# The head of a two-layer trunk: its first two output pairs run tile by tile together, and the dt chain moves up behind the sums of squares

## The chip, the cores and the metric

One NeuronCore of a Trainium2 chip runs the whole program. The metric is the device time of one execution in microseconds; the kernel before and the changed one compute the same numbers. Engines go by these names: TensorE (PE in the rows; PEld its weight loads), VectorE (DVE), ScalarE (ACT), GpSimd (POOL) and SyncE (SP, whose queue issues most transfers).

## The reference, cut to what matters

Two residual layers over x, 512 positions by 1024 channels. Layer 0 mixes tokens with a Mamba-2 state-space block, layer 1 with a convolution module; each is followed by a gated MLP. Only the start of layer 0 matters here:

```python
u = rms_norm(h, norm_mix[0])                 # h = x
zxbcdt = u @ in_proj                         # 1024 -> 2048 (z) + 4096 (x, B, C) + 32 (dt)
z, xbc, dt = split(zxbcdt)
xbc = silu(causal_dwconv(xbc, conv_w, conv_b))          # width 4
dt = softplus(dt + dt_bias)
acs = cumsum(dtc * a, axis=1)                # within chunks of 128 positions, a = -exp(a_log)
scores = cb[..., None] * exp(seg) * dtc      # seg: differences of acs, causal
y_diag = einsum(scores, xc); y_off = einsum(cc, state) * exp(acs)
```

The norm's factor rstd is one number for each position, so it can be applied after the product with `in_proj`.

## The kernel before

Channels lie on the 128 partitions and the 512 positions in the free dimension: x is eight tiles of 128x512 (`xin[0..7]`, 256 KB each). Each float32 operand of a large product is split into a rounded half and a remainder, and three matmuls (`L308` to `L310`) stand for one product. x is split by `split_x` (ScalarE makes the high half at L242, VectorE the low half at L243), weights by `Weights._make` (GpSimd the high half at L125, VectorE the low half at L127).

**Units and pairs.** An output pair is two tiles of 128 output channels, each summed in one PSUM bank; the pool of these banks, `mm`, has four. `in_proj` has 24 pairs. A unit `(kind, pair, k)` is the part of a pair that x tiles k and k+1 give: 2 tiles by 2 outputs by 3 matmuls, twelve. Pair `in` 0 has units (0,0), (0,2), (0,4), (0,6), and so on. `weight_units` lists all units in the order of use; `Weights.get` hands them out in that order and makes units up to four ahead. A unit's weights are 256 KB. Two successive units of one pair come in one load of 512 KB, except that the first two units of all are loaded alone. The loads land in `wraw` (three buffers), the split halves lie in `whi` and `wlo` (five buffers each).

**The head.** SP issues, in this order: tile 0, unit 0's weights, tile 1, unit 1's weights, tiles 2 and 3, the weights up to unit 3, tiles 4 to 7, the weights up to unit 5, then five constants (`dtw`, `parc`, `con`, `dtp`, `par`). All x tiles are split and squared (`SqSum.add`, the sum on VectorE at L285). Then the loop over eight head groups g starts. In group 0 it runs pair 0 (B and C of the group), pair 1 (the group's x) and pair 2 (its z), one after the other.

**The sums and rstd.** `start_rstd` (called in the hook behind pair 0's fourth unit) issues the dt products (sixteen records, eight tiles) into the bank `dps` (L357), then `SqSum.rstd`: the sum of squares is split in two (L239, L240), two products with ones add it over the channels (L294, L295), a root (L297) and a reciprocal on VectorE (L298) give `rstd`.

**Freeing a bank.** `scaled` multiplies a bank by rstd into a `u` tile (L337; six `u` tiles in all), which frees the bank. `conv4` then makes the convolution from `u` into `cv` tiles (L429, L433, L439; eight `cv` tiles, which also hold x at the start).

**The dt chain.** `dt_chain` (called behind pair 1's convolution) multiplies `dps` by rstd (L371, into a `u` tile), folds its four partial sums with a product on TensorE (L373), and then goes back and forth between VectorE and ScalarE on 32 partitions: v (L378), absolute value, exponential, o (L383), logarithm (L385), L386, L387, dt (L389), the scan to `acs` (L395), `nac`, and the decay weights (L407 to L409). Six of its results are `u` tiles: dv, v, e, o, dt and nac. On SP it issues the writes of `acs`, `nac` and `dec` to DRAM and the read back of `dec`. `dt_transposes` and the first `load_acs` (both in group 1's first hook) use what it leaves; `core` of group 0 has four stages, of which `stage_a` needs the loaded `ab` and makes exponentials from it, `stage_b` multiplies with them on TensorE (L509), and `stage_c` multiplies with the states (L532).

**What sets the order.** The program's order gives each instruction its rank; a planner lays out the order on each engine from it, and takes a later instruction first where by its own times an earlier one is not ready. The order on an engine is then fixed, and semaphores make each instruction wait for its operands. A tile's buffer is given out by the same planner.

Of the kernel before, what the change touches and what calls it, by code (L numbers as in the profile page):

```python
# [20 lines left out]
KD = D // P  # L21
NG = 8
# [20 lines left out]
    _n += _w  # L43
NCOL = _n

KINDS = {"in": KD, "out": DI // P, "up0": KD, "dn0": NF, "pw1": KD, "pw2": KD, "up1": KD, "dn1": NF}


def weight_units():
    seq = []  # L50

    def pair(kind, p, k0=0, k1=None):
        k1 = KINDS[kind] if k1 is None else k1
        seq.extend((kind, p, k) for k in range(k0, k1, 2))

    def two(kind, p, k0, k1):
        for k in range(k0, k1, 4):
            for q in (p, p + 1):
                seq.extend((kind, q, kk) for kk in range(k, min(k + 4, k1), 2))

    for g in range(NG):
        pair("in", 3 * g)
        if g == 5:
            for p in range(4):
                pair("out", p, 0, 8)
        pair("in", 3 * g + 1)
        if g != 1:
            pair("in", 3 * max(g - 1, 0) + 2)
    pair("in", 3 * 7 + 2)
    two("out", 0, 8, 16)  # L70
    pair("out", 2, 8, 16)
    pair("out", 3, 8, 16)

    def ffn(i):
        for a, b in FPARTS:
            for p in range(a, b):
                pair(f"up{i}", p)
            for p in range(4):
                pair(f"dn{i}", p, a, b)

    ffn(0)
    for p in range(8):
        pair("pw1", p)
    two("pw2", 0, 0, 8)
    pair("pw2", 2)
    pair("pw2", 3)
    ffn(1)
    return seq
# [54 lines left out]
def trunk(ctx, tc, a, out):  # L143
    nc = tc.nc
# [13 lines left out]
    W = Weights(tc, nc, a, wr, ws, 4)  # L158
# [10 lines left out]
    def mm_tile():  # L169
        return pm.tile([P, T], F32, name="mm", tag="mm")  # L170
# [25 lines left out]
    xin = [cv_tile() for _ in range(KD)]  # L196
# [1 line left out]
    W.fill(1)  # L198
    nc.sync.dma_start(xin[1], a["x"][1])
    W.fill(2)  # L200
    nc.sync.dma_start(xin[2], a["x"][2])
    nc.sync.dma_start(xin[3], a["x"][3])
    W.fill(3)
    for k in range(4, KD):
        nc.sync.dma_start(xin[k], a["x"][k])
    W.fill(5)
    dtw = cst.tile([P, KD, NH], F32, name="dtw")
    nc.sync.dma_start(dtw, a["dtw"])
    lo_c, hi_c = _COLS["cw"], _COLS["dsk"]
# [91 lines left out]
    def mm_unit(ps, key, xs, k0, k1):  # L301
        kind, p, k = key
        whi, wlo = W.get(key)
        for kk in range(2):
            xhi, xlo = xs[k + kk - k0]
            for m in range(2):
                c = slice(m * P, (m + 1) * P)
                pe.matmul(ps[m], lhsT=whi[:, kk, c], rhs=xhi, start=(k + kk == k0), stop=False)  # L308
                pe.matmul(ps[m], lhsT=wlo[:, kk, c], rhs=xhi, start=False, stop=False)  # L309
                pe.matmul(ps[m], lhsT=whi[:, kk, c], rhs=xlo, start=False, stop=(k + kk == k1 - 1))  # L310

    def mm_pair(kind, p, xs, k0=0, k1=None, hooks=None):
        k1 = KINDS[kind] if k1 is None else k1
        ps = [mm_tile(), mm_tile()]
        for i, k in enumerate(range(k0, k1, 2)):
            mm_unit(ps, (kind, p, k), xs, k0, k1)
            if hooks and i in hooks:
                hooks[i]()
        return ps
# [13 lines left out]
    def scaled(ps, r):  # L333
        us = []
        for q in ps:
            u = u_tile()
            dve.tensor_tensor(u, q, r, op=ALU.mult)  # L337
            us.append(u)
        return us
# [3 lines left out]
    xs = []  # L343
# [8 lines left out]
    state = {}  # L352

    def start_rstd():
        for k in range(KD):
            j = k % 4
            pe.matmul(dps[NH * j : NH * (j + 1), :], lhsT=dtg[:, k, :], rhs=xin[k], start=(k < 4), stop=(k >= 4))  # L357
        state["r"] = sq.rstd(D)
# [9 lines left out]
    def dt_chain():  # L368
        r = state["r"]
        dv = u_tile()  # L370
        dve.tensor_tensor(dv, dps, r, op=ALU.mult)  # L371
        vps = c_tile()
        pe.matmul(vps[0:NH, :], lhsT=mask32, rhs=dv, start=True, stop=True)  # L373
        v = u_tile()[0:NH, :]
        na = cst.tile([NH, 1], F32, name="na")
        act.activation(na, dtp[:, 1:2], AF.Exp)
        dve.tensor_scalar(na, na, -1.0, None, op0=ALU.mult)
        dve.tensor_scalar(v, vps[0:NH, :], dtp[:, 0:1], None, op0=ALU.add)  # L378
        e = u_tile()[0:NH, :]
        act.activation(e, v, AF.Abs)  # L380
        act.activation(e, e, AF.Exp, scale=-1.0)
        o = u_tile()[0:NH, :]
        dve.tensor_scalar(o, e, 1.0, None, op0=ALU.add)  # L383
        l = cv_tile()[0:NH, :]
        act.activation(l, o, AF.Ln)  # L385
        dve.scalar_tensor_tensor(o, in0=o, scalar=1.0, in1=e, op0=ALU.subtract, op1=ALU.subtract)  # L386
        dve.tensor_tensor(l, l, o, op=ALU.subtract)  # L387
        dt = u_tile()[0:NH, :]
        dve.scalar_tensor_tensor(dt, in0=v, scalar=0.0, in1=l, op0=ALU.max, op1=ALU.add)  # L389
        da = cv_tile()[0:NH, :]  # L390
        dve.tensor_scalar(da, dt, na, None, op0=ALU.mult)
        acs = cv_tile()[0:NH, :]
        for c in range(NCH):
            b = slice(c * P, (c + 1) * P)
            dve.tensor_tensor_scan(  # L395
                acs[:, b], ones[0:NH, :], da[:, b], 0.0, op0=ALU.mult, op1=ALU.add
            )
        nc.sync.dma_start(acs_d, acs)
        nac = u_tile()[0:NH, :]
        dve.tensor_scalar(nac, acs, -1.0, None, op0=ALU.mult)  # L400
        nc.sync.dma_start(nac_d, nac)
        wend = cv_tile()[0:NH, :]
        dec = cst.tile([NH, NCH], F32, name="dec")
        for c in range(NCH):
            b = slice(c * P, (c + 1) * P)
            last = acs[:, (c + 1) * P - 1 : (c + 1) * P]
            act.activation(wend[:, b], nac[:, b], AF.Exp, bias=last)  # L407
            act.activation(dec[:, c : c + 1], last, AF.Exp)
        dve.tensor_tensor(wend, wend, dt, op=ALU.mult)  # L409
        nc.sync.dma_start(dec_d, dec)  # L410
        nc.sync.dma_start(
            decb.rearrange("p h c -> p (h c)"),
            dec_d.rearrange("h c -> (h c)").partition_broadcast(P),
        )
        state["dt"] = (dt, acs, wend)
# [29 lines left out]
    def load_acs(g):  # L445
        ab = ab_tile()
        nc.sync.dma_start(
            ab[:, 0:4, :].rearrange("p h t -> p (h t)"),
            acs_d[4 * g : 4 * g + 4, :].rearrange("h t -> (h t)").partition_broadcast(P),
        )  # L450
        nac = nac_d[4 * g : 4 * g + 4, :].rearrange("(j q) t -> q j t", q=2)
        for q in range(2):
            nc.sync.dma_start(ab[64 * q : 64 * q + 64, 4:6, :], nac[q].partition_broadcast(64))
        return ab
# [102 lines left out]
    def z_evac(ps):  # L557
        zs = scaled(ps, state["r"])
        for z in zs:
            act.activation(z, z, AF.Silu)  # L560
        return zs

    state["ysq"] = SqSum()
    ysplit = Acts()
    prev = None

    def nop():
        pass

    for g in range(NG):  # L570
        if prev:
            st, sa, sb, sc, sd = prev
        hk = {}
        if g == 0:
            hk = {3: start_rstd}
        elif g == 1:
            def first():
                dt_transposes()
                prev[0]["acs"] = load_acs(0)
            hk = {0: first, 1: sa}  # L580
        else:
            hk = {0: sa}
        ps = mm_pair("in", 3 * g, xs, hooks=hk)
        bm, cm = conv4(scaled(ps, state["r"]), (16 + g, 24 + g), state["exp"] if g == 1 else None)
        if g == 5:
            for p in range(4):
                ps = mm_pair("out", p, ysplit, 0, 8)
                for m in range(2):
                    act.activation(h[2 * p + m], ps[m], AF.Copy)
            del ysplit[:8]  # L590
        ps = mm_pair("in", 3 * g + 1, xs, hooks={0: sb, 3: sc} if prev else None)
        x0, x1 = conv4(scaled(ps, state["r"]), (2 * g, 2 * g + 1))
        if g == 0:
            dt_chain()
        else:
            acs = load_acs(g)
        if prev:
            if g > 1:
                zs = z_evac(mm_pair("in", 3 * (g - 1) + 2, xs))
            sd(zs)  # L600
        else:
            zs = z_evac(mm_pair("in", 2, xs))
        prev = core(g, bm, cm, x0, x1)
        if g:
            prev[0]["acs"] = acs
    st, sa, sb, sc, sd = prev
    xre = []
    ps = mm_pair("in", 23, xs, hooks={0: sa, 3: sb})
    zs = z_evac(ps)
# [37 lines left out]
    for p in (2, 3):  # L647
        ps = mm_pair("out", p, ysplit, 8, 16)
# [451 lines left out]
```

## Time and profile before

| | us |
|---|---|
| median of three runs | 1327.25 (1326.42 to 1330.48) |
| profiled execution | 1330.38 |
| its span, first to last instruction | 1328.5 |
| TensorE matmuls busy | 1313.5 |
| VectorE busy | 1009.5 |
| ScalarE busy | 427.9 |
| GpSimd busy | 349.5 |

The span is that of the profiled execution's own instructions. The page gives busy times by engine, the timeline gives single instructions with the time the engine stood idle before them and what ended it, and the list of waits sums these by who was waited for. Matmuls are pipelined, so a matmul's duration in a row (0.39) is longer than the step from one start to the next.

### The profile page before, as it was taken

How to read it: one execution, taken by the hardware profiler on the slowest of the kernel's cores; microseconds unless marked ns; L12 is line 12 of the kernel's file. 1: busy time of each engine (PE TensorE's matmuls, PEld its weight loads, DVE VectorE, ACT ScalarE, POOL GpSimd, SP SyncE). 2: the span in 40 equal slices, each digit the busy share in tenths (PEclk: the TensorE clock that was granted, in tenths of full speed). 3: DMA queues.
4: the chain of work that ended last, by engine and by line, in shares of the span. 5: the costliest groups of instructions: out<-in, count | busy, mean ns of one | idle time of the engine just before them, and what ended most of it. 6: DMA issues, size and time to landing. Idle time of an engine off the chain costs nothing. (4 is left out here: it accounts for less than half of the span.)

```text
span 1328.5 us, 17161 instructions
## 1 busy us (share of the span) xinstructions
PE 1313.5 (99%) x6302; PEld 1068.7 (80%) x6302; DVE 1009.5 (76%) x1516; ACT 427.9 (32%) x694; POOL 349.5 (26%) x475
## 2 busy tenths in 40 slices
PE   8999999999999999999999999999999999999998
PEld 5778788888888888888888887667888888888887
DVE  7889797378989977388739879998787637763774
ACT  4586545145322322033203332225332102210224
POOL 3322122222223223233223321221222222222220
PEclk9999999999999999999999999999999999999999
DMA  6364323334243345357636659991333323333321
GB/s 215 113 179 127 128 98 125 95 112 143 79 126 96 96 141 177 111 202 245 204 114 220 228 185 269 255 226 47 99 95 96 95 95 96 98 102 99 98 80 64
DMA packets 56228, 181.77 MB, mean 137 GB/s; under 512 B 7248, under 2 KB 8016, under 8 KB 53072
## 3 DMA queue, kind: packets, MB, share of 16 engines
q1 hardware_dynamic: 49680, 152.28, 36.9%
q0 software_dynamic: 5744, 28.12, 6.6%
q8 instruction: 50, 0.82, 0.3%
q10 hardware_dynamic: 720, 0.27, 0.1%
q14 instruction: 34, 0.28, 0.1%
HBM read 159.28 MB, written 20.85 MB: 136 GB/s over the span
## 5 line engine op out<-in xcount | busy, mean ns | idle before, releaser
L125 POOL TENSOR_SCALAR whi<-wraw 128x512 fp32r<-128x512 f32 x408 | 315.6, 774 | 846.2 <-PE mm L310 579.9
L308 PE MATMUL mm<-xs,whi 128*128 128x512 f32 x1216 | 475.5, 392 | 1.1 <-POOL whi L125 0.7
L309 PE MATMUL mm<-xs,wlo 128*128 128x512 f32 x1216 | 473.9, 390 | 0.4 <-DVE wlo L127 0.4
L310 PE MATMUL mm<-xs,whi 128*128 128x512 f32 x1216 | 473.3, 391 | 0.5 <-DVE xs L243 0.5
L127 DVE TENSOR_TENSOR wlo<-wraw,whi 128x512 fp32r<-128x512 f32 x408 | 285.4, 703 | 210.3 <-POOL whi L125 208.6
L308 PEld LDWEIGHTS mm<-xs,whi 128*128 128x128 f32 x1216 | 228.1, 188 | 54.3 <-issue 2.9
L310 PEld LDWEIGHTS mm<-xs,whi 128*128 128x128 f32 x1216 | 228.0, 188 | 50.9 <-DVE xs L243 2.0
L309 PEld LDWEIGHTS mm<-xs,wlo 128*128 128x128 f32 x1216 | 228.1, 188 | 48.6 <-DVE wlo L127 1.3
L308 PE MATMUL mm<-as,whi 128*128 128x512 f32 x532 | 207.0, 390 | 1.7 <-ACT as L263 1.7
L309 PE MATMUL mm<-as,wlo 128*128 128x512 f32 x532 | 207.1, 389 | 0.0
L310 PE MATMUL mm<-as,whi 128*128 128x512 f32 x532 | 203.7, 389 | 0.2 <-DVE as L268 0.2
L699 ACT ACTIVATE cv<-u,par 128x512 f32<-128x512 f32 x88 | 67.2, 809 | 361.8 <-DVE u L337 361.8
L703 DVE SCALAR_TENSOR_TENSOR cv<-u,par,cv 128x510 f32<-128x510 f32 (+1 forms) x176 | 136.2, 834 | 0.2 <-ACT cv L699 0.2
L337 DVE TENSOR_TENSOR u<-mm,rstd 128x512 f32<-128x512 f32 x152 | 102.5, 688 | 28.2 <-PE mm L310 27.3
L308 PEld LDWEIGHTS mm<-as,whi 128*128 128x128 f32 x532 | 99.9, 188 | 22.7 <-ACT as L263 1.9
L310 PEld LDWEIGHTS mm<-as,whi 128*128 128x128 f32 x532 | 99.8, 188 | 21.3 <-DVE as L268 0.6
L309 PEld LDWEIGHTS mm<-as,wlo 128*128 128x128 f32 x532 | 99.9, 188 | 20.7
L433 DVE SCALAR_TENSOR_TENSOR cv<-u,parc,cv 128x511 f32<-128x511 f32 (+2 forms) x96 | 75.5, 816 | 5.4 <-ACT cv L429 5.4
L707 ACT ACTIVATE cv<-cv 128x512 f32<-128x512 f32 x44 | 27.8, 633 | 80.5 <-DVE cv L703 80.4
L718 DVE TENSOR_TENSOR h<-h,mm 128x512 f32<-128x512 f32 x46 | 30.9, 687 | 25.2 <-PE mm L310 25.1
L239 ACT ACTIVATE as<-cv 128x512 fp32r<-128x512 f32 x44 | 27.9, 634 | 51.6 <-DVE cv L708 50.8
L476 ACT ACTIVATE ab<-ab,acT 128x128 f32<-128x128 f32 x128 | 38.6, 388 | 13.5 <-DMA ab<-acs_d 13.5
(188 smaller groups left out, 995.6 us busy)
## 6 DMA issues: line engine op xcount, KB each, us to landing
wraw<-up_dram SPq DMA_DIRECT2D x88, 512.0 KB, 3.7
wraw<-in_dram SPq DMA_DIRECT2D x47, 512.0 KB, 3.8
wraw<-dn_dram SPq DMA_DIRECT2D x40, 512.0 KB, 3.6
pw1s<-ab POOLq DMA_DIRECT2D x14, 1024.0 KB, 4.4
ab<-acs_d SPq DMA_DIRECT2D x8, 1024.0 KB, 5.5
wraw<-out_dram SPq DMA_DIRECT2D x16, 512.0 KB, 3.9
ab<-pw_dram SPq DMA_DIRECT2D x16, 512.0 KB, 4.6
wlo<-pw1s SPq DMA_DIRECT2D x28, 256.0 KB, 4.8
```

Of the source, the lines that this page charges most:

```text
L125: nc.gpsimd.tensor_scalar(hi, t, 1.0, 1.0, op0=ALU.mult, op1=ALU.mult)
L127: nc.vector.tensor_tensor(lo, t, hi, op=ALU.subtract)
L239: act.activation(hi, src, AF.Copy)
L308: pe.matmul(ps[m], lhsT=whi[:, kk, c], rhs=xhi, start=(k + kk == k0), stop=False)
L309: pe.matmul(ps[m], lhsT=wlo[:, kk, c], rhs=xhi, start=False, stop=False)
L310: pe.matmul(ps[m], lhsT=whi[:, kk, c], rhs=xlo, start=False, stop=(k + kk == k1 - 1))
L337: dve.tensor_tensor(u, q, r, op=ALU.mult)
L433: dve.scalar_tensor_tensor(o[:, d:], in0=u[:, : T - d], scalar=col("cw", 4 * i + 3 - d), in1=o[:, d:], op0=ALU.mult, op1=ALU.add,)
L476: act.activation(e, e, AF.Relu, bias=acT[:, c, 4 * g + j : 4 * g + j + 1], scale=-1.0)
L699: act.activation(o, u, AF.Identity, scale=col(f"fw{i}", 3 * j + 2), bias=col(f"fb{i}", j))
L703: dve.scalar_tensor_tensor(o[:, d:], in0=u[:, : T - d], scalar=col(f"fw{i}", 3 * j + 2 - d), in1=o[:, d:], op0=ALU.mult, op1=ALU.add,)
L718: dve.tensor_tensor(h[2 * p + m], h[2 * p + m], ps[m], op=ALU.add)
```

## The change

A list `HEAD` gives the order of the eight units of pairs 0 and 1. Both pairs run in it before anything else: the units of tiles 0 and 1 for both pairs, those of tiles 2 and 3 for both, then the rest of pair 0 and the rest of pair 1. `weight_units` and the issue order of the tiles follow it; tiles 4 and 5 now come before the fourth unit's weights, tiles 6 and 7 after them. Behind the sixth unit (the last of pair 0) stand `start_rstd` and, directly behind it, `dt_chain`. After the eight units come both convolutions, pair 2 and group 0's `core`; the loop starts at group 1 and is otherwise the same.

```diff
--- before.py
+++ after.py
@@ -43,6 +43,7 @@
     _n += _w
 NCOL = _n
 
+HEAD = ((0, 0), (1, 0), (0, 2), (1, 2), (0, 4), (0, 6), (1, 4), (1, 6))
 KINDS = {"in": KD, "out": DI // P, "up0": KD, "dn0": NF, "pw1": KD, "pw2": KD, "up1": KD, "dn1": NF}
 
 
@@ -59,11 +60,14 @@
                 seq.extend((kind, q, kk) for kk in range(k, min(k + 4, k1), 2))
 
     for g in range(NG):
-        pair("in", 3 * g)
-        if g == 5:
-            for p in range(4):
-                pair("out", p, 0, 8)
-        pair("in", 3 * g + 1)
+        if g == 0:
+            seq.extend(("in", p, k) for p, k in HEAD)
+        else:
+            pair("in", 3 * g)
+            if g == 5:
+                for p in range(4):
+                    pair("out", p, 0, 8)
+            pair("in", 3 * g + 1)
         if g != 1:
             pair("in", 3 * max(g - 1, 0) + 2)
     pair("in", 3 * 7 + 2)
@@ -198,12 +202,10 @@
     W.fill(1)
     nc.sync.dma_start(xin[1], a["x"][1])
     W.fill(2)
-    nc.sync.dma_start(xin[2], a["x"][2])
-    nc.sync.dma_start(xin[3], a["x"][3])
-    W.fill(3)
-    for k in range(4, KD):
-        nc.sync.dma_start(xin[k], a["x"][k])
-    W.fill(5)
+    for n, ks in ((3, (2, 3)), (4, (4, 5)), (5, (6, 7))):
+        for k in ks:
+            nc.sync.dma_start(xin[k], a["x"][k])
+        W.fill(n)
     dtw = cst.tile([P, KD, NH], F32, name="dtw")
     nc.sync.dma_start(dtw, a["dtw"])
     lo_c, hi_c = _COLS["cw"], _COLS["dsk"]
@@ -562,18 +564,21 @@
 
     state["ysq"] = SqSum()
     ysplit = Acts()
-    prev = None
-
-    def nop():
-        pass
-
-    for g in range(NG):
-        if prev:
-            st, sa, sb, sc, sd = prev
+    ps = [[mm_tile(), mm_tile()], [mm_tile(), mm_tile()]]
+    for i, (p, k) in enumerate(HEAD):
+        mm_unit(ps[p], ("in", p, k), xs, 0, KD)
+        if i == 5:
+            start_rstd()
+            dt_chain()
+    bm, cm = conv4(scaled(ps[0], state["r"]), (16, 24))
+    x0, x1 = conv4(scaled(ps[1], state["r"]), (0, 1))
+    zs = z_evac(mm_pair("in", 2, xs))
+    prev = core(0, bm, cm, x0, x1)
+
+    for g in range(1, NG):
+        st, sa, sb, sc, sd = prev
         hk = {}
-        if g == 0:
-            hk = {3: start_rstd}
-        elif g == 1:
+        if g == 1:
             def first():
                 dt_transposes()
                 prev[0]["acs"] = load_acs(0)
@@ -588,21 +593,14 @@
                 for m in range(2):
                     act.activation(h[2 * p + m], ps[m], AF.Copy)
             del ysplit[:8]
-        ps = mm_pair("in", 3 * g + 1, xs, hooks={0: sb, 3: sc} if prev else None)
+        ps = mm_pair("in", 3 * g + 1, xs, hooks={0: sb, 3: sc})
         x0, x1 = conv4(scaled(ps, state["r"]), (2 * g, 2 * g + 1))
-        if g == 0:
-            dt_chain()
-        else:
-            acs = load_acs(g)
-        if prev:
-            if g > 1:
-                zs = z_evac(mm_pair("in", 3 * (g - 1) + 2, xs))
-            sd(zs)
-        else:
-            zs = z_evac(mm_pair("in", 2, xs))
+        acs = load_acs(g)
+        if g > 1:
+            zs = z_evac(mm_pair("in", 3 * (g - 1) + 2, xs))
+        sd(zs)
         prev = core(g, bm, cm, x0, x1)
-        if g:
-            prev[0]["acs"] = acs
+        prev[0]["acs"] = acs
     st, sa, sb, sc, sd = prev
     xre = []
     ps = mm_pair("in", 23, xs, hooks={0: sa, 3: sb})
```

## Rows read from the trace of the kernel before

**Rows 1.** The page, busy time (share of the span) and instructions of each engine.

```profile
PE 1313.5 (99%) x6302; PEld 1068.7 (80%) x6302; DVE 1009.5 (76%) x1516; ACT 427.9 (32%) x694; POOL 349.5 (26%) x475
```

**Rows 2.** Stretches: us; PE, PEld, DVE, ACT, POOL busy (instructions); granted clock; DMA share, GB/s.

```profile
5.76:20.08 14.32, 13.32 (x51) 8.67 (x51) 14.32 (x19) 8.70 (x15) 6.37 (x7) 1.00 0.86 306
...
56.65:100.00 43.35, 41.70 (x233) 33.99 (x233) 38.33 (x66) 34.28 (x70) 13.84 (x11) 1.00 0.59 175
```

**Rows 3.** Timeline of TensorE in the head: start, duration, instruction, idle before and releaser.

```profile
5.76 0.73 PE L308 MATMUL mm<-xs,whi 128*128 128x512 f32 x2 [0.68 <-POOL whi L125]
...
7.72 0.39 PE L308 MATMUL mm<-xs,whi 128*128 128x512 f32 x1
...
13.34 0.73 PE L309 MATMUL mm<-xs,wlo 128*128 128x512 f32 x2 [0.39 <-DVE wlo L127]
14.61 0.73 PE L310 MATMUL mm<-xs,whi 128*128 128x512 f32 x2 [0.53 <-DVE xs L243]
...
20.08 1.92 PE L357 MATMUL pc<-cv,dtg 128*32 128x512 f32 x16
21.93 0.50 PE L309 MATMUL mm<-xs,wlo 128*128 128x512 f32 x1
...
27.34 0.39 PE L295 MATMUL pc<-sq,ones_r 128*128 128x512 f32 x1
...
28.71 0.39 PE L310 MATMUL mm<-xs,whi 128*128 128x512 f32 x1
...
32.79 0.39 PE L310 MATMUL mm<-xs,whi 128*128 128x512 f32 x1
33.48 0.47 PE L308 MATMUL mm<-xs,whi 128*128 128x512 f32 x1 [0.31 <-DVE u L337]
...
40.25 1.05 PE L373 MATMUL pc<-u,con 128*32 128x512 f32 x2
41.23 0.50 PE L310 MATMUL mm<-xs,whi 128*128 128x512 f32 x1
```

**Rows 4.** Timeline of VectorE, end of the sums to the first freed banks.

```profile
24.18 0.68 DVE L240 TENSOR_TENSOR sq<-sqs,sq 128x512 fp32r<-128x512 f32 x1
...
28.85 3.35 DVE L298 RECIPROCAL rstd<-rstd 128x512 f32<-128x512 f32 x1
...
32.66 2.47 DVE L337 TENSOR_TENSOR u<-mm,rstd 128x512 f32<-128x512 f32 x4
35.05 0.68 DVE L371 TENSOR_TENSOR u<-pc,rstd 128x512 f32<-128x512 f32 x1
```

**Rows 5.** TensorE's waits, whole run, then first 120 us: total us, times, longest.

```profile
PE pc L532 <- DVE state L524: 2.8, 2, 2.3
...
PE pc L509 <- DVE ab L497: 1.2, 3, 0.4
...
PE pc L532 <- DVE state L524: 0.5, 1, 0.5
```

**Rows 6.** Timeline of GpSimd, its third and fourth start on weights.

```profile
10.69 2.06 POOL L125 TENSOR_SCALAR whi<-wraw 128x512 fp32r<-128x512 f32 x2 [3.11 <-DMA wraw<-in_dram]
14.74 1.91 POOL L125 TENSOR_SCALAR whi<-wraw 128x512 fp32r<-128x512 f32 x2 [2.00 <-DMA wraw<-in_dram]
```

**Rows 7.** Transfers of the first 40 us by line: count, KB each, median us to landing.

```profile
wraw<-in_dram SPq DMA_DIRECT2D x8, 512.0 KB, 5.0
...
wraw<-in_dram SPq DMA_DIRECT2D x2, 256.0 KB, 4.1
```

**Rows 8.** Timeline of ScalarE, the root for rstd.

```profile
27.77 0.69 ACT L297 ACTIVATE rstd<-pc,eps_r 128x512 f32<-128x512 f32 x1 [2.75 <-PE pc L295]
```

**Rows 9.** Waits of SP's queue in the first 60 us.

```profile
SPq L398 <- DVE cv L395: 7.2, 1, 7.2
```

**Rows 10.** Timeline of VectorE, two steps of the dt chain.

```profile
44.17 0.73 DVE L378 TENSOR_SCALAR u<-pc,dtp 32x512 f32<-32x512 f32 x1
...
52.43 0.68 DVE L386 SCALAR_TENSOR_TENSOR u<-u 32x512 f32<-32x512 f32 x1 [2.26 <-ACT cv L385]
```

## The prediction

> **What bounds the kernel now.** I read the page first: TensorE's matmuls are busy 1313.5 of 1328.5 us [rows 1]. So the time is TensorE's work plus some 15 us in which it has none, and a change that adds and removes no matmul can move only that rest. Next come the stretches: the granted clock is 1.00 in the head and in the first head group's stage, so the clock costs nothing there, and in the head VectorE is busy without a gap and the DMA engines are 0.86 busy at 306 GB/s [rows 2]. Third, TensorE's own timeline of the head. From its first real matmul at 5.76 to the first one of the third output pair at 33.48 pass 27.72 us [rows 3]. The work in them: 96 matmuls of the first two pairs at 0.227 us from start to start (eighteen steps from 28.71 to 32.79), 21.8 us; the dt products, 20.08 to 21.93, 1.85 us; two sums for rstd, 0.46 us; 24.1 in all [rows 3]. So 3.6 us are lost: 0.6 in the first six matmuls (1.96 us instead of 1.36); 2.4 from 7.72 to 20.08, where 44 matmuls (50 ahead of the dt products [rows 2], less the six) take 12.36 us instead of 10.0, around waits for a weight's low half at 13.34 and for an x tile's low half at 14.61; and 0.47 before 33.48, where the third pair waits for a bank [rows 3]. The first two pairs fill all four banks of the matmul pool, and a bank is freed by the multiplication by rstd on VectorE, so that last wait hangs on rstd: its reciprocal runs from 28.85 to 32.20, and the multiplications follow from 32.66 at 0.6 us each [rows 4]. What else the change can reach lies in the stage of the first head group: three waits for `ab`, 1.2 us, and one for `state`, 0.5 us [rows 5].
>
> **Part 1, the order of the units.** A unit is twelve matmuls, 2.72 us. Before, two x tiles fed one unit before the next two were wanted; now tiles 0 to 3 feed two units per two tiles. Nothing is added but one weight load: the first eight units came in five loads (two of 256 KB, three of 512) and come in six (four and two). Does the new order keep TensorE fed? The loads come in the order issued, so I count bytes. Before, 2.0 MB were there when GpSimd could start on the third load at 10.69, and 3.5 MB at 14.74 [rows 6]. Now unit (1,2) is complete at 2.5 MB, a third of the way, 12.0; its split takes 1.0 on GpSimd [rows 6] and 0.7 on VectorE, so 13.7, and TensorE, with the 0.6 us of its start and three units done, wants it at 14.5. Units (0,4) and (0,6) are complete at 3.5 MB as before, 14.74, split by 16.4 and 17.4, and wanted at 17.3 and 20.0. The x tiles are wanted at half the pace. SP issues in order: the load of (1,2) needs the raw buffer of (0,0), and tiles 6 and 7, the next weights and five constants are queued behind it; that buffer is free once the very first weight split is done, which TensorE's first unit needs anyway. So I take the 2.4 us as gone, keep 0.6 for the start and 0.4 for edges: the 96 matmuls and the dt and rstd products end at 5.76 + 24.1 + 1.0 = 30.9, where they ended at 33.0.
>
> The load that is split in two speaks against this. In the rows 512 KB land after 5.0 us and 256 KB after 4.1 [rows 7], so two small loads one after the other would take 3.2 us more than one large one; but loads overlap here, and the stretch moved 306 GB/s with them [rows 2]. I cost the extra load at nothing, covered by the 0.8 us of slack of unit (1,2), and its other end, 3.2 us, is rival D. The Trainium skill ("DMA: Bandwidth & Descriptors", section "Anatomy of one DMA — SWDGE (gpsimd) path") gives each DMA a fixed cost of about 2.0 us whatever its size; uncovered, that would make the forecast below 1326.3, and no run here shows that cost alone.
>
> **Part 2, sums, rstd and the dt chain.** `start_rstd` moves from behind the fourth unit to behind the sixth, and `dt_chain` from behind the second pair's convolution to directly behind it. VectorE's work up to the sum of squares is the same, so the sum's low half is ready where it is now, 24.18 + 0.68 = 24.86 [rows 4]. The second rstd product ran only at 27.34 [rows 3], 2.5 us later, for its place in TensorE's queue; the root started 0.43 after it [rows 8] and the reciprocal took 3.35 [rows 4]. Now TensorE has 72 matmuls and the dt products behind it at 5.76 + 0.6 + 16.3 + 0.3 + 1.85 = 24.8, so the rstd products can come at 25 to 26. With 1.5 us from the product to the reciprocal (27.34 to 28.85) and 3.35 for that, rstd is there at 30.5 (bounds: 29.75 with the product at 24.9; 32.2 if it keeps its old time). Then VectorE does the dt product with rstd first, 0.68 [rows 4], to 31.2, and the first two multiplications to 31.8 and 32.4. Late next is rstd: TensorE is done at 30.9 and waits. But the fold of the dt products (L373), which held a full TensorE from 40.25 to 41.23 [rows 3], is ready at 31.2 and runs in that wait. So the third pair starts at 32.4 with the fold done; before, that point was 33.48 + 0.98 = 34.46. Gain 2.1; bounds 0.4 (rstd at 32.2, start at 34.05) and 2.6 (the fold from 30.9 to 31.9).
>
> The rest of the chain: each of its VectorE and ScalarE steps now stands ahead of both convolutions in program order, but TensorE wants the next banks only 22 us later, two pairs of 10.9. Its writes of `acs`, `nac` and `dec` on SP wait for VectorE with weight loads queued behind; before, SP stood 7.2 us so [rows 9] and TensorE did not notice, since split weights for units ahead were there. Without that cover a load comes 7.2 us late. The chain's later part moves up: its fold goes from 40.25 to about 31.2, and the load of `ab`, the exponentials and with them the waits of [rows 5] hang on its end, so they have about 9 us more. Those waits, 1.66 us, can go whole, or a wait as long as the longest of the kind, 2.3 us [rows 5], can stand in their place: gain 1.66 to loss 0.7. I take half of what is there, 0.8, because the order on each engine is laid out anew and such a wait occurs in a later group without this cause.
>
> **Sum.** 2.1 + 0.8 = 2.9 us off the profiled execution's 1330.4 (span 1328.5 and 1.9 around it): 1327.5. That execution is 3.1 us above the median of the runs, 1327.25; the same 2.9 off the median gives 1324.3.
>
> **Rivals.** A: the wait only changes its name. If rstd comes no earlier, what the feed gives back turns into a longer wait for a bank; 0.4 stays, from the fold, and the time is 1326.8. For it: rstd hangs on VectorE, full from 5.76 to 20.08 [rows 2]. Against: the 2.5 us between 24.86 and 27.34. That the change does not do what it says goes here too: TensorE's order is not the program's alone (before, the dt products ran behind 50 matmuls, 51 instructions with the first of them [rows 2], where the program has them behind 48), and if it comes out much as it is, nothing moves.
>
> B: everything comes. Head 2.6, the first group's 1.66, half a us of the later wait of that kind: 4.8, so 1322.5. For it: that wait of 2.3 us [rows 5] stands in an order that is made anew. Against: nothing in the change aims at it.
>
> C: slower. The chain needs six `u` tiles, the multiplications that free the banks need `u` tiles too, and there are six. If the chain, first in the program, holds all but one, the second multiplication waits until L386 has run and given up its inputs. From v at 44.17 to the end of L386 at 53.11 are 8.9 us [rows 10]. Then the second bank comes at rstd + 0.7 + 1.0 + 8.9 + 0.7, 11.3 us, instead of 1.9, and TensorE stands 9.4 us more: 1333.7. It decides from the point at which tiles are given to the chain before its steps can run. Against: v, e, o and dt are written one after another over those 9 us, so a tile that is given when it is first written leaves room.
>
> D: the extra load shows. Unit (1,2) comes 3.2 us later, 2.4 beyond its slack; TensorE ends at 33.3, behind rstd, the third pair starts with the fold done at 34.3, and the head's gain is 0.2: 1326.2 with the 0.8 of the first group.
>
> **How the numbers follow.** Forecast 0.43, A 0.20, B 0.25, C 0.07, D 0.05. A measurement of this kernel tells about 0.3%, 4.0 us, from no change: faster is under 1323.3, slower over 1331.2. Three quarters of B are faster, and so is the forecast where its terms come near their upper bounds, a quarter of its cases: 0.30. C is slower: 0.07. The rest, 0.63, is within. Range: from 1320.5 (B with the whole 2.3 us of the later wait) to 1328.5 (A with a wait in the first group's stage that is 0.7 longer, and a us of the runs' own spread); C and a tenth of the others lie outside.
>
> **What would show it.** Part 1: after the first unit no wait for x or weights over 0.3 us up to the dt products; wrong would be a wait for a weight split before unit (1,2) near 14.5 (D). Part 2: the second rstd product at 25 to 26, the reciprocal's end near 30.5, the fold before the third pair, whose first matmul is near 32.4. A: the reciprocal's end at 32 and a wait of over a us for `u`. C: a wait of several us there, with L386 just before its end. First group: the waits of the `ab` and `state` products together under 0.9 us. The forecast falls if TensorE's idle time outside the head changes by more than 1.5 us.

## The result: slower, since the banks are freed only behind the whole dt chain

| | before | changed |
|---|---|---|
| median of the first runs, us | 1326.88 (4 runs, 1326.42 to 1330.48) | 1336.26 (4 runs, 1336.16 to 1337.53) |
| ratio, 95% interval | | 1.0067 (1.0048 to 1.0086) |
| a second series, us | 1330.17 (18 runs) | 1335.25 (7 runs), 1.0046 (1.0029 to 1.0063) |
| profiled execution, span, us | 1330.38, 1328.5 | 1336.16, 1334.3 |

The ratios are taken over all executions of a series and are not quite the quotient of the two medians; one of the seven, 1905.56 us at a mean granted clock of 0.652, is left out of its ratio. The kernel before varies more from one execution to the next (1324.9 to 1333.8 over all series), so medians are compared only within a series. The profiled execution of before is among the longer ones of its series; its span lies only 5.8 us under that of the changed kernel.

The page's busy times of the changed kernel, beside [rows 1]: TensorE has 1.4 us more, though it runs the same 6302 matmuls.

```profile
PE 1314.9 (99%) x6302; PEld 1071.3 (80%) x6302; DVE 1010.7 (76%) x1516; ACT 425.3 (32%) x692; POOL 343.0 (26%) x475
```

TensorE's timeline of the changed kernel in the head, beside [rows 3]:

```profile
5.58 0.73 PE L310 MATMUL mm<-xs,whi 128*128 128x512 f32 x2 [0.42 <-POOL whi L129]
...
18.18 1.92 PE L359 MATMUL pc<-cv,dtg 128*32 128x512 f32 x16 [0.45 <-DVE dtg L348]
...
25.39 0.39 PE L297 MATMUL pc<-sq,ones_r 128*128 128x512 f32 x1
...
30.85 0.39 PE L312 MATMUL mm<-xs,whi 128*128 128x512 f32 x1
31.90 1.05 PE L375 MATMUL pc<-u,con 128*32 128x512 f32 x2 [0.66 <-DVE u L373]
40.46 0.63 PE L423 MATMUL pc<-con,u 32*128 32x32 f32 x4 [7.51 <-DVE u L391]
41.41 1.26 PE L423 MATMUL pc<-con,cv 32*128 32x32 f32 x4 [0.33 <-DVE cv L397]
43.50 0.77 PE L310 MATMUL mm<-xs,whi 128*128 128x512 f32 x1 [0.83 <-DVE u L339]
44.06 0.63 PE L311 MATMUL mm<-xs,wlo 128*128 128x512 f32 x1
...
49.17 0.40 PE L311 MATMUL mm<-xs,wlo 128*128 128x512 f32 x1
49.41 0.39 PE L312 MATMUL mm<-xs,whi 128*128 128x512 f32 x1
```

Up to 31.90 the times are close to the forecast: after the first matmul there is no wait for x or a weight's half ahead of the dt products, the eight units are done at 31.1, and the fold (now L375) runs in the wait for rstd. Then TensorE stands: 7.5 us ahead of the transposes of the dt chain (L423), which the planner had put in front of the third pair, and another 0.8 for a multiplication into a `u` tile (L339), which frees the bank. This last wait is the one that lets the pair start. The third pair starts at 43.50 instead of 33.48 [rows 3]. Its first steps, 44.06 on, are 0.43 us long instead of 0.23. VectorE says why; its timeline in the same stretch, beside [rows 4]:

```profile
27.36 3.35 DVE L300 RECIPROCAL rstd<-rstd 128x512 f32<-128x512 f32 x1
...
31.17 0.68 DVE L373 TENSOR_TENSOR u<-pc,rstd 128x512 f32<-128x512 f32 x1
...
32.98 0.74 DVE L380 TENSOR_SCALAR u<-pc,dtp 32x512 f32<-32x512 f32 x1 [0.31 <-PE pc L375]
36.35 0.42 DVE L385 TENSOR_SCALAR u<-u 32x512 f32<-32x512 f32 x1 [2.63 <-ACT u L383]
38.30 0.68 DVE L388 SCALAR_TENSOR_TENSOR u<-u 32x512 f32<-32x512 f32 x1 [1.52 <-ACT cv L387]
...
42.34 0.41 DVE L402 TENSOR_SCALAR u<-cv 32x512 f32<-32x512 f32 x1
42.68 2.47 DVE L339 TENSOR_TENSOR u<-mm,rstd 128x512 f32<-128x512 f32 x4
```

The reciprocal (L300) ends at 30.71, the dt product (L373) follows at 31.17, and then come only steps of the chain, with VectorE idle 2.63 and 1.52 us between them, until nac (L402) is written at 42.34. All four multiplications (L339) that free the banks run behind that, from 42.68. They had rstd and finished banks since 31.

The stretches show the clock (columns as in [rows 2]): from the fold's end to the third pair's start, the pair's first matmuls, and what follows.

```profile
32.90:43.50 10.60, 1.92 (x10) 1.24 (x9) 6.19 (x13) 7.26 (x13) 0.00 (x0) 0.62 0.14 47
43.50:49.20 5.70, 5.70 (x14) 4.47 (x15) 5.70 (x10) 3.02 (x6) 0.00 (x0) 0.50 0.54 202
49.20:56.65 7.45, 7.45 (x34) 6.17 (x33) 6.93 (x10) 3.85 (x5) 3.47 (x3) 1.00 1.05 281
```

TensorE was busy 1.92 of 10.60 us, and the granted clock fell to its lower level, 1.2 of 2.4 GHz: 0.50 in the next 5.70 us. The 13 steps from 43.50 to 49.17 took 5.67 us; at 0.227 they take 2.95. The same matmul in both traces, worked out from the timelines, gives the balance: the third pair's first starts 10.0 us later than before, its 25th 12.65 later. From 155 us on every one starts 5.9 later, to the end. So 6.8 us came back in between. Of these, 4.0 are waits for `ab` and `state` that only the execution of before has (1.2 and 2.8 us), and some 2 are the fold and eight transposes, which the changed kernel had already run before its third pair; the rest was not traced.

### The profile page after: what moved, and what is told of

It reads as the page before. It is cut to its first block, busy times and chain, and to the rows that moved or that the text cites. A ratio compares the mean times of both kernels' runs of the same rounds, so it can differ in the third digit from the quotient of the medians.

```text
span 1334.3 us, 17178 instructions
## 1 busy us (share of the span) xinstructions
PE 1314.9 (99%) x6302; PEld 1071.3 (80%) x6302; DVE 1010.7 (76%) x1516; ACT 425.3 (32%) x692; POOL 343.0 (26%) x475
## 5 line engine op out<-in xcount | busy, mean ns | idle before, releaser
L129 POOL TENSOR_SCALAR whi<-wraw 128x512 fp32r<-128x512 f32 x408 | 309.1, 758 | 854.6 <-PE mm L312 576.9
L339 DVE TENSOR_TENSOR u<-mm,rstd 128x512 f32<-128x512 f32 x152 | 102.4, 687 | 29.2 <-PE mm L312 28.5
L716 DVE TENSOR_TENSOR h<-h,mm 128x512 f32<-128x512 f32 x46 | 30.9, 686 | 25.2 <-PE mm L312 25.1
L287 DVE TENSOR_TENSOR sqs<-sqs,sq 128x512 f32<-128x512 f32 x54 | 41.0, 759 | 0.8 <-ACT sq L286 0.4
```

The costliest lines, as they stand in the source:

```text
L129: nc.gpsimd.tensor_scalar(hi, t, 1.0, 1.0, op0=ALU.mult, op1=ALU.mult)
L287: self.last = dve.tensor_tensor(self.t, self.t, s, op=ALU.add)
L716: dve.tensor_tensor(h[2 * p + m], h[2 * p + m], ps[m], op=ALU.add)
```

## The experiments

The theories. Theory 1, handing out: buffers of one name go to their writers in the program's order, so a multiplication's `u` tile is given only after the chain's last one, nac. Theory 2, count: six `u` tiles are too few (rival C as the prediction put it). Theory 3, rank: VectorE takes the chain first because it stands first, whatever its tiles are.

**The two parts alone.** The pairs' order without the chain's move:

```diff
         if i == 5:
             start_rstd()
-            dt_chain()
     bm, cm = conv4(scaled(ps[0], state["r"]), (16, 24))
     x0, x1 = conv4(scaled(ps[1], state["r"]), (0, 1))
+    dt_chain()
```

> Part 1 alone: the eight units in the new order, the sums and rstd behind the sixth, but the dt chain behind both convolutions, as before. All theories on the chain say that the loss is gone: the multiplications at rstd, near 30.7, the third pair near 31.6 instead of 33.48, the fold later on a full TensorE as before, so 1.9 us less than before: 1325 (1323 to 1327). If the new order of the units is itself the cause of the loss, the time is over 1330.

Measured: 1325.87 us against 1329.55, 0.9970 (0.9958 to 0.9981). TensorE in the head and its largest waits in the whole run (us in total, times, longest):

```profile
31.45 0.47 PE L310 MATMUL mm<-xs,whi 128*128 128x512 f32 x1 [0.29 <-DVE u L339]
...
38.23 1.04 PE L375 MATMUL pc<-u,con 128*32 128x512 f32 x2
```

```profile
PE mm L310 <- ACT as L265: 1.7, 1, 1.7
PE mm L194 <- DVE eps_l L235: 1.6, 1, 1.6
PE pc L359 <- DVE dtg L348: 0.6, 1, 0.6
PE pc L840 <- DVE cv L800: 0.4, 1, 0.4
PE mm L310 <- DVE u L339: 0.3, 1, 0.3
```

These are all of its waits. The third pair starts at 31.45, 2.0 us earlier than before, and the waits for `ab` and `state` of [rows 5] are not in this execution at all. The order of the units is a gain.

The chain's move without the pairs' order (the old loop, with `dt_chain` in pair 0's fourth hook, directly behind `start_rstd`):

```diff
+            def first_sums():
+                start_rstd()
+                dt_chain()
-            hk = {3: start_rstd}
+            hk = {3: first_sums}
...
-        if g == 0:
-            dt_chain()
-        else:
+        if g:
             acs = load_acs(g)
```

> Part 2 alone: the units in the old order, the sums behind the fourth unit, the dt chain directly behind them. Theories 1, 2 and 3 all say: the multiplications wait for the chain, the third pair starts near 45, part of it at half clock, and the time is that of the changed kernel plus the two us of the feed, 1338 (1335 to 1340). If it takes both parts together to make the loss, it is near 1327.

Measured: 1336.58 us, 1.0053 (1.0036 to 1.0070). The same wait, 1.7 us later:

```profile
33.56 1.05 PE L373 MATMUL pc<-u,con 128*32 128x512 f32 x2 [0.21 <-DVE u L371]
42.16 0.63 PE L421 MATMUL pc<-con,u 32*128 32x32 f32 x4 [7.55 <-DVE u L389]
...
45.21 0.77 PE L308 MATMUL mm<-xs,whi 128*128 128x512 f32 x1 [0.83 <-DVE u L337]
```

So the loss is the chain's move: it appears with the move alone and is absent without it. The two parts do not simply add. The expectation had this kernel 2 us above the changed one, but its ratio, 1.0053, lies between the changed kernel's two, 1.0046 and 1.0067; of the 1.7 us at the third pair's start 0.5 is left at the end of the two profiled executions.

**Which of the three theories.** First the chain's six `u` results in two tiles of the `as` pool:

```diff
-        dv = u_tile()
+        k1 = ap_.tile([P, 4, T], F32, name="as", tag="as")
+        k2 = ap_.tile([P, 4, T], F32, name="as", tag="as")
+        dv = k1[:, 0, :]
...
-        nac = u_tile()[0:NH, :]
+        nac = k2[0:NH, 1, :]
```

> The changed kernel, but the six results of the dt chain that were `u` tiles (dv, v, e, o, dt, nac) lie in two tiles of the `as` pool, which nothing else uses yet. In the changed kernel the four multiplications that free the banks ran only from 42.68, behind the whole chain, although rstd was there at 30.71. Theory 1 (handing out): tiles of one name are given out in the program's order, so the multiplications' `u` tiles came after nac, the chain's last. Theory 2 (count): six `u` tiles were too few. Both say: the multiplications run right behind the dt product, at about 31.8, the third pair starts near 33, the granted clock stays at 1.00, and the time is some 11 us under the changed kernel's, about 1325 (1322 to 1328). Theory 3 (rank): VectorE takes the chain's steps first because they stand first, whatever tiles they use: the multiplications stay behind nac and the time stays near 1336.

Measured: 1330.17 us, 1.0009 (0.9997 to 1.0021). The head came out as theories 1 and 2 said: the multiplications ran at 31.92, the third pair started at 33.03 with the fold done, the clock stayed up. Theory 3 falls for the multiplications. VectorE, then TensorE:

```profile
31.92 2.47 DVE L339 TENSOR_TENSOR u<-mm,rstd 128x512 f32<-128x512 f32 x4
```

```profile
33.03 0.50 PE L310 MATMUL mm<-xs,whi 128*128 128x512 f32 x1
```

But the time missed the expected 1325 by 5 us: TensorE now waited later, in the first group's stage, for the silu of the convolutions. TensorE there, then ScalarE:

```profile
67.25 1.16 PE L468 MATMUL pc<-cv 128*128 128x128 f32 x8 [2.24 <-ACT cv L443]
...
74.59 0.66 PE L472 MATMUL pc<-con,cv 128*128 128x128 f32 x4 [3.02 <-ACT cv L443]
```

```profile
50.84 1.28 ACT L411 ACTIVATE cv<-as,cv 32x128 f32<-32x128 f32 x4
52.03 2.55 ACT L433 ACTIVATE cv<-u,parc 128x512 f32<-128x512 f32 x4
...
65.86 1.95 ACT L443 ACTIVATE cv<-cv,parc 128x512 f32<-128x512 f32 x3
...
73.82 0.72 ACT L443 ACTIVATE cv<-cv,parc 128x512 f32<-128x512 f32 x1
```

The convolutions' first step (L433, into `cv` tiles) ran at 52.03, right behind wend (L411), the chain's last `cv` result. That is theory 1's pattern on another name.

Then the dose: only dt and nac leave the `u` tiles, so that o is the chain's last there.

```diff
-        dt = u_tile()[0:NH, :]
+        k2 = ap_.tile([P, 4, T], F32, name="as", tag="as")
+        dt = k2[0:NH, 0, :]
...
-        nac = u_tile()[0:NH, :]
+        nac = k2[0:NH, 1, :]
```

> The changed kernel, but only dt and nac lie in the `as` pool; dv, v, e and o stay `u` tiles. Theory 1: the last of the chain's `u` tiles is now o, written at about 36.8 by L385, so the multiplications start then instead of at 42.68, the third pair at about 37.6 instead of 43.5: 6 us less, or more where the clock stays up, 1330 (1328 to 1332). Theory 2: four of six tiles are the chain's, two are free, and the first two multiplications run right behind the dt product: 1325. Theory 3: no change, 1336.

Measured: 1332.53 us, 1.0022 (1.0008 to 1.0036). VectorE:

```profile
36.37 0.41 DVE L385 TENSOR_SCALAR u<-u 32x512 f32<-32x512 f32 x1 [2.63 <-ACT u L383]
36.72 1.87 DVE L339 TENSOR_TENSOR u<-mm,rstd 128x512 f32<-128x512 f32 x3
38.51 0.67 DVE L388 SCALAR_TENSOR_TENSOR u<-u 32x512 f32<-32x512 f32 x1
...
39.83 0.67 DVE L339 TENSOR_TENSOR u<-mm,rstd 128x512 f32<-128x512 f32 x1
```

The multiplications run directly behind o (L385), three at once, and the third pair starts at 37.53. The time is 0.5 us above the range that theory 1 gave. Two `u` tiles had been free since rstd was there, so count alone does not explain it. Count shows too, but behind the order: when o is written, v, e and o hold three of the six tiles, three multiplications run, and the fourth follows at 39.83, when e and o have been read for the last time. The opposite test, more tiles in the same order:

```diff
-        return wt("u", bufs=6)
+        return wt("u", bufs=10)
...
-    ap_ = ctx.enter_context(tc.tile_pool(name="ap", bufs=5))
+    ap_ = ctx.enter_context(tc.tile_pool(name="ap", bufs=4))
```

> The changed kernel with ten `u` tiles instead of six, and four `as` tiles instead of five to make room. It tells a shortage of tiles from the order in which they are given out. Theory 2 (count): with four more tiles the multiplications run right behind the dt product at about 31.9, and the third pair starts near 33. Theory 1 (handing out in program order): nothing changes in the head, the multiplications follow nac at about 42.7, the third pair starts near 43.5, and the time is near 1336.

Measured: 1334.86 us, a single execution, so without an interval; what counts here is the order in its trace. Nothing moved in the head:

```profile
42.28 0.41 DVE L402 TENSOR_SCALAR u<-cv 32x512 f32<-32x512 f32 x1
42.62 2.46 DVE L339 TENSOR_TENSOR u<-mm,rstd 128x512 f32<-128x512 f32 x4
```

Four more tiles are there from the start, and the multiplications still follow nac (L402). Theory 2 falls, theory 1 stands. It says what to do: give the chain's four `cv` results (l, da, acs, wend) tiles of their own as well.

```diff
-        l = cv_tile()[0:NH, :]
+        l = k2[0:NH, 2, :]
...
-        wend = cv_tile()[0:NH, :]
+        wend = k3[0:NH, 1, :]
```

> The kernel with own tiles for dv, v, e, o, dt and nac, and own tiles (`as` pool) for the chain's four `cv` results too (l, da, acs, wend). With the `u` tiles freed, the wait in the head was gone but TensorE then waited 3.0 and 2.2 us in the first group's stage for the silu of the convolutions, whose first step (into `cv` tiles) ran only at 52.03, right behind wend. Theory 1 (handing out): `cv` tiles are given out in the program's order too, so now the convolutions start right behind the multiplications, at about 34, the two waits vanish, and the early chain costs nothing: 1324 (1321 to 1327). Theory 3 (rank): the chain's steps hold ScalarE and VectorE by their rank; the convolutions stay late and the time stays near 1330.

Measured: 1325.29 us against 1329.03, 0.9970 (0.9960 to 0.9980). ScalarE and TensorE's largest waits:

```profile
32.74 2.56 ACT L434 ACTIVATE cv<-u,parc 128x512 f32<-128x512 f32 x4 [5.96 <-DVE u L339]
35.78 0.63 ACT L384 ACTIVATE as<-as 32x512 f32<-32x512 f32 x1 [0.48 <-DVE as L382]
...
42.42 0.72 ACT L444 ACTIVATE cv<-cv,parc 128x512 f32<-128x512 f32 x1 [0.41 <-DVE cv L438]
```

```profile
PE mm L310 <- ACT as L265: 1.7, 1, 1.7
PE mm L194 <- DVE eps_l L235: 1.6, 1, 1.6
PE pc L377 <- DVE as L375: 0.6, 1, 0.6
PE pc L537 <- DVE state L529: 0.5, 1, 0.5
```

The convolutions start at 32.74 and the chain goes on between them; the waits for silu are gone. The change as it was meant, with the chain's results out of the way, is a gain of 3.7 us on before and, by the ratios, of some 10 to 13 on the changed kernel.

**Is the chain's early place worth anything?** The chain behind both convolutions, with own tiles for its six `u` results and, in another kernel, for all ten:

> Own tiles for dv, v, e, o, dt and nac as above, but the chain behind both convolutions, as before the change; the pairs in the new order. It tells what the chain's early place is worth once the tiles are not in the way: against the kernel with all own tiles and the early chain, this one shows the gain of the place alone. Theory: the first group's stage has no wait over 1 us with either, so the place is worth nothing: 1325, within 2 us of the kernel with the pairs' order alone (0.997 of before). If the early chain is worth something, this one is 2 us or more above the one with all own tiles.

Measured: 1326.86 us, 0.9984 (0.9972 to 0.9996). That is 1.6 us above the kernel with ten own tiles and the early chain in the same series, under the 2 us that would have spoken for the early place; but that kernel differs in the tiles of the `cv` results too. In the next one the place alone differs.

> Own tiles for all ten results of the chain, the chain behind both convolutions, the pairs in the new order. Against the kernel with all own tiles and the early chain (0.997 of before) this differs in the chain's place alone. Theory: its place is worth nothing, since either stands clear of the first group's stage: 0.997, within 0.002. If the early place pays once no tile is in its way, this one is 0.999 or above.

Measured: 1326.76 us, 0.9977 (0.9965 to 0.9990), against 0.9970 (0.9960 to 0.9980) with the early place. The intervals overlap, and 0.9970 is also what the pairs' order alone gives. An advantage of the early place, if there is one, is under 0.3%.

**What the half clock costs.** Idle matmuls (nobody reads their sum) behind the fold, first 32:

```diff
             dt_chain()
+            fill_ps = c_tile()
+            for n in range(32):
+                pe.matmul(fill_ps, lhsT=ones_r, rhs=xs[7][0], start=True, stop=True)
```

> The changed kernel with 32 more matmuls of 512 columns, whose sum nobody reads, ranked behind the dt chain, so that they lie in the wait behind the fold (7.3 us at 0.227). It measures what the clock costs: in the changed kernel the granted clock is 0.50 from 35.5 to 49.15, and the first fourteen matmuls of the third pair take 0.427 instead of 0.227 us each. If that is the idle time's doing, the clock stays at 1.00, these matmuls take 0.227, and the time is 2.8 us under the changed kernel's, 1333.4 (1332 to 1335). If the slow matmuls have another cause, nothing changes: 1336.

Measured: 1334.83 us, 1.0041 (1.0028 to 1.0054). The time lies in the expected range, but the clock did not stay up, so this is inconclusive: in the profiled execution, the longest of the eight, rstd came 1.5 us later, the matmuls ended 3 us ahead of the third pair, and the granted clock was 0.50 again from 46.17. So 44 of them, beside a repeat of the changed kernel:

> The changed kernel once more, beside the others of this call and the same executions of the kernel before, since the kernel before stood at medians of 1326.88 and 1329.55 in two calls. Expected: 1336 (1335.5 to 1337), and a ratio to before between 1.0048 and 1.0086, as at first.

> The changed kernel with 44 idle matmuls behind the fold instead of 32: 10.0 us, so that TensorE has almost no wait from the fold at 32.9 to the third pair near 43.5. With 32 of them 2 us of waits were left and the granted clock still fell, from 46.17 to 49.59. If the half clock comes from the waits, the clock stays at 1.00 here, the third pair's first matmuls take 0.227, and the time is 2.7 us under that of the changed kernel in this call (2.0 to 3.0). If it comes from something else in the third pair's start, it is still 0.50 there and the time is the changed kernel's.

Measured: changed kernel 1335.25, 1.0046 (1.0029 to 1.0063), so below the ratio that was expected of it; with 44 idle matmuls 1335.33, 1.0048 (1.0030 to 1.0065). The stretches of the kernel with 44, columns as in [rows 2], then the repeat's from the third pair's start:

```profile
32.90:43.90 11.00, 11.00 (x53) 8.69 (x52) 6.53 (x13) 7.60 (x14) 0.00 (x0) 1.00 0.14 47
43.90:49.60 5.70, 5.70 (x28) 4.69 (x27) 5.70 (x10) 2.69 (x5) 2.05 (x1) 1.00 0.61 219
```

```profile
43.10:48.80 5.70, 5.70 (x17) 4.53 (x18) 5.70 (x10) 3.02 (x6) 0.00 (x0) 0.65 0.53 206
```

With TensorE busy the clock stays at 1.00, and 24 matmuls of the third pair take 5.6 us instead of 7.4 in the repeat: the half clock is the waits' doing. But the time is the same, and the expected 2.7 us are not there. By the timelines of the two profiled executions, only 1.8 us were to be had, since the repeat's clock was at 0.50 for a shorter time (0.65 on average). The kernel with the idle matmuls starts the pair 0.9 later, about half of it because rstd came 0.5 later, and so leads by 0.9 after 24 matmuls. It loses 1.3 near 119 us, at a wait of 1.0 us for `state` that the repeat does not have. Whether that wait comes from the idle matmuls is not shown.

## Why the prediction was wrong

It forecast 1324.3 (1320.5 to 1328.5) and gave slower 0.07; measured were 1336.26 and 1335.25. The lower end of the range comes out as 1320.7 from its own terms; nothing hangs on that.

**Part 1 was right.** The eight units ended at 31.1 (forecast 30.9), 2 us before their old end, with no wait for x or weights after the first matmul. The extra load showed nowhere (D): GpSimd and VectorE had unit (1,2) ready in time (its splits started at 11.58 and 13.74). The Trainium skill ("DMA: Bandwidth & Descriptors", section "Anatomy of one DMA — SWDGE (gpsimd) path") gives its fixed cost of about 2.0 us for transfers on the path of GpSimd; these loads are issued on SP, and TensorE waited for no weight here after its first. The kernel with the pairs' order alone gained 3.7 us, of which 2.0 stand in the head.

**Part 2 was right up to the dt product.** The second rstd product ran at 25.39 (25 to 26), the reciprocal ended at 30.71 (30.5). The fold came at 31.90 instead of 31.2, for a weight's split stood ahead on VectorE. The dt products ran at 18.18, long before the 72nd matmul, where the prediction had them; the planner had put them there, and TensorE waited 0.45 us for their weights (`dtg`).

**The step that failed** is the next one: "and the first two multiplications to 31.8 and 32.4". They came at 42.68. Rival C named the place, the `u` tiles, but gave it 0.07 and dismissed it with "a tile that is given when it is first written leaves room". That a tile is given when it is written may be so; what the runs bear out is that no writer gets a tile while one that stands earlier in the program has not got its own. So the wait does not end with L386 (L388 in the changed kernel, done at 38.98), which gives inputs up, but with nac (42.34 to 42.75), and all four multiplications wait, the first too. That C's price, 1333.7, came within 2.6 us was luck: from v to the end of that step the chain took 6.0 us, not 8.9, and C left out the steps from there to nac, 3.4 to 3.8 us.

The trace of before has the same pattern. VectorE there, around the third pair's own multiplications:

```profile
57.72 0.42 DVE L400 TENSOR_SCALAR u<-cv 32x512 f32<-32x512 f32 x1
58.06 1.27 DVE L337 TENSOR_TENSOR u<-mm,rstd 128x512 f32<-128x512 f32 x2
```

The third pair was finished when the fourth began, at 45.7, rstd was there, VectorE was idle for 2.26 us before L386 at 52.43 [rows 10], and yet its multiplications (L337) ran at 58.06, directly behind nac (L400). It cost nothing there, because TensorE had two other banks and then transposes to do. Two of the experiments show that the names do this too: with the pairs' order alone the third pair's multiplications ran from 56.04, directly behind nac; with the same order and own tiles for the six `u` results they ran from 46.81, long before nac at 57.35. The prediction read only the first four multiplications [rows 4], which ran at once; they stood ahead of the chain in the program.

**The clock** was not a term at all. It was right that the head of before lost nothing to it; waits of 8.7 us together made it a cost: over the third pair's first 24 matmuls 2.6 us in the first profiled execution and 1.8 in the repeat. That it shows in the time is not borne out: the idle matmuls took it away and the time stayed.

**First group's waits.** The forecast of 0.8 us was of the right sign, but the reason given for it is not borne out. In the profiled execution of the changed kernel none of the waits of [rows 5] is left, neither the 1.7 us of the first 120 us nor the 2.3 us later on; so TensorE's idle time outside the head changed by 4.0 us, and by the prediction's own sign (1.5 us) it falls here as well. The waits do not follow the chain's place: with the chain late before has 4.0 us of them, the pairs' order alone none, and the two kernels with own tiles 2.0 and 0.7; with the chain early they lie between none and 1.4. What puts them into one execution and not into another was not settled; they may be why before's times spread by 9 us.

**Rivals.** A (rstd not earlier) did not come true: rstd came 1.5 us earlier. B (everything comes) did not come true in the changed kernel; the kernel with ten own tiles goes that way, with 3.7 of its 4.8 us. C had the right side and the right place, with another rule. D did not come true.

## What to carry to other kernels

When a block of work is moved up in the program, list the names of the buffers it takes and ask who behind it takes buffers of the same names: here the order of handing out made four short multiplications wait for a chain of 11 us, although their operands were there and VectorE stood idle in between. To see it in a trace before, look for an instruction whose operands have long been there, on an idle engine, directly behind another writer of the same name. Give a latency-bound side chain tiles of its own; then its place hardly matters.

## What was not expected of the hardware

The granted clock fell to 0.50 at 35.5, while TensorE stood behind the fold, and was back at 1.00 at 49.15, within the third pair. With idle matmuls in the same place it stayed at 1.00, and yet the program's time stayed too: 1335.33 against 1335.25 us.
